# Conditioning products moved from VectorE to GpSimd, their row sums to ScalarE

## The chip, the cores and the metric

The kernel runs on one core of a Trainium2 chip. A core has five engines with instruction queues of their own: TensorE (PE in the profile, with its weight loads as PEld), VectorE (DVE), ScalarE (ACT), GpSimd (POOL) and SyncE (SP), which here only issues DMAs. Each queue runs in order; engines wait for one another by semaphores. The metric is the device time of one execution in microseconds, lower is better, as the median of several runs.

## The reference

A two-layer backbone over 256 latent and 256 context tokens of width 1024. Layer 0 mixes tokens with a bidirectional mLSTM, layer 1 with latent attention; a gated convolutional FFN follows each. What this change touches is the modulation: six vectors of width 1024 per layer and condition, from a matrix-vector product with the SiLU of a condition row. There are two conditions, `c` for the latents and `c_ctx` for the context.

```python
def _modulation(cond, w, b):
    m = jax.nn.silu(cond) @ w + b
    return jnp.split(m[:, None, :], 6, axis=-1)
...
        ml = _modulation(c, ada_w[i], ada_b[i])
        mc = _modulation(c_ctx[None, :], ada_w[i], ada_b[i])
        hl = _modulate(x, ml[0], ml[1])
...
        x = _layer_norm(ALPHA * x + ml[2] * yl, ln_g[i, 0], ln_b[i, 0])
```

## The kernel before

**Matrix products.** All weights are float32 and stream from memory in tiles of 128 x 1024. SyncE loads a tile (`raw`), ScalarE casts it to a high part (L345), VectorE subtracts that from the tile to get a low part (L368), and TensorE makes three products of high and low parts (L430, L433, L434). There are three buffers for the pair of parts (`NB = 3`, tile `w`); some tiles go to larger spare buffers instead (`wu`). A tile serves 24 matmuls of 512 columns in most stages and 12 in `mout`. The stages in order: start-up, `up`, `og`, the value products, `qk` (with the mLSTM heads' softmax-like work beside it), `mout`, the first FFN's `fin0` and its second product, layer 1's attention, `fin1`, `fout1`.

**The modulations.** Shift and scale of layer 0's mixer (chunks 0 and 1) are made in the start-up by TensorE. The rest are made later, in the background, without TensorE: the transposed matrix comes in tiles of 128 outputs x 1024 inputs (`ar`, L567), and for each condition VectorE multiplies a tile with the condition's SiLU row, broadcast to all partitions (`bc`), and accumulates along the row in the same instruction (`scalar_tensor_tensor` with `accum_out`, L544). The product itself goes to `junk` and is not read. One such instruction is a step. There are 128 steps on 80 tiles: chunks 2 and 3 (half) of layer 0 in `up` and `og`, 24 steps; the rest from `qk` to `fin0`, 104 steps. Layer 1's chunks 2 to 5 need only the latents' condition, so there a tile has one step, else two. After each chunk an addition of the bias follows (L549), and for the gates (chunks 2 and 5) a transposition and a store, since they are read back as rows.

**What sets the order.** The program is written as one sequence; a planner orders each engine's queue by that sequence and its own estimate of durations. Background work is kept in generators that are advanced at fixed places: `tick(n, n2)` advances the modulations by `n2` steps, kept as a running sum, after each weight tile. `ADA_U`, `ADA_T`, `ADA_Q`, `ADA_M` and `ADA_F` are these rates in `up`, `og`, `qk`, the first 22 tiles of `mout` and `fin0`. So that the planner does not run a step ahead of its place, `gate` (L559) lets ScalarE copy one element of the weight tile used last into the place that the step will write. `ar` tiles use three buffers (two of tag `ar`, one `ar1`), two loaded ahead at first. GpSimd otherwise issues DMAs (stores of `up`'s results, loads for heads and residuals) and makes two products at the very end (L1252, L1253).

Of the kernel before, what the change touches and what calls it, by code (L numbers as in the profile page):

```python
# [7 lines left out]
F32 = mybir.dt.float32  # L8
F32R = mybir.dt.float32r
I32 = mybir.dt.int32  # L10
AF = mybir.ActivationFunctionType
ALU = mybir.AluOpType
# [33 lines left out]

VE = {1: (3, 0), 2: (3, 0), 3: (3, 0)}

ADA_U, ADA_T, ADA_Q, ADA_M, ADA_F = 1.4, 1.3, 1.6, 0.6, 1.25

NUP = 5
# [345 lines left out]
class K:  # L401
# [127 lines left out]
    def ada_bg(self, l, c, k0, k1, nconds):  # L529


        nc = self.nc
        if c in (2, 5):
            v = self.adav
            col = v[:, 0:8 * nconds].rearrange("p (j k) -> p k j", k=8)
        else:
            col = self.modc[l, c][:, :, 0:nconds]
        for k in range(k0, k1):
            w = self.art.pop(0)
            self.ar_load()  # L540
            for j in range(nconds):
                o = self.pool.tile([128, 1024], F32, tag="junk", name="junk", bufs=1)
                self.gate(col[0:1, k, j:j + 1])
                nc.vector.scalar_tensor_tensor(o, w, 1.0, self.bc[j], op0=ALU.mult, op1=ALU.mult,  # L544
                                               accum_out=col[:, k, j:j + 1])
                yield
        b = self.smc("ada_c")[:, 48 * l + 8 * c + k0:48 * l + 8 * c + k1].unsqueeze(2).to_broadcast([128, k1 - k0, nconds])
        col = col[:, k0:k1]
        nc.vector.scalar_tensor_tensor(col, col, 1.0 if c in (1, 4) else 0.0, b, op0=ALU.add, op1=ALU.add)  # L549
        if c in (2, 5):  # L550
            t = self.pool.tile([128, 32], F32, tag="adat", name="adat", bufs=1)
            nc.vector.transpose(t, v)
            for q in range(4):
                nc.sync.dma_start(self.gd[l, c].rearrange("j (k q i) -> q (j k) i", q=4, i=32)[q, 0:8 * nconds],
                                  t[32 * q:32 * q + 8 * nconds])

    def gate(self, ap):

        self.nc.scalar.copy(ap, self.st.last[0:1, 0:1].bitcast(F32))  # L559
# [10 lines left out]
    def ada_all(self, items):  # L570

        nc = self.nc
        self.bc = []
        for j in range(2):
            r = self.pool.tile([128, 1024], F32, tag="acc", name="bc", bufs=2)
            self.gate(r[0:1, 0:1])
            nc.sync.dma_start(r, self.a["crow"][j:j + 1, :].to_broadcast([128, 1024]))
            self.bc.append(r)
        self.arq = [(l, c, k) for l, c, k0, k1 in items for k in range(k0, k1)]
        self.art, self.nar = [], 0  # L580
        for _ in range(2):
            self.ar_load()
        for _ in range(2):
            yield
        for r in self.bc:
            nc.scalar.activation(r, r, AF.Silu)  # L586
        yield
        for l, c, k0, k1 in items:
            yield from self.ada_bg(l, c, k0, k1, 2 if l == 0 or c < 2 else 1)
        self.bc = None  # L590


# [1770 lines left out]
```

## Time and profile before

| what | value |
|---|---|
| median of 3 runs | 1346.83 us (1346.54 to 1347.15) |
| span of the profiled execution, first to last instruction | 1345.3 us |
| TensorE, VectorE, ScalarE, GpSimd busy | 99%, 79%, 53%, 11% of the span |
| mean granted clock of TensorE | 0.998 |
| steps of the modulations (L544) | 128, the first at 63.0 us, the last at 866.2 us |

The profiled execution's own time is not listed apart from its span; the median of the runs lies 1.5 us above the span. Busy times of two engines overlap, so shares do not add up. Matmuls are pipelined, so a busy TensorE is judged by the distance between the starts of two matmuls. In a group's row stand the line, engine, operation, tiles and shapes, count, busy us, mean ns of one, and behind the second bar the engine's idle time before it with what ended it.

### The profile page before, as it was taken

What the parts mean: (1) busy time and instruction counts of PE and PEld (TensorE: products, weight loads), DVE (VectorE), ACT (ScalarE), POOL (GpSimd) and SP (SyncE); (2) the same over time, 40 slices, a digit from 0 to 9 for tenths busy, and PEclk for the clock granted to TensorE, in tenths of its full rate; (3) what the DMA queues carried; (4) which work ended last, traced back from release to release, by engine and by line L of the source; (5) the groups of instructions that cost most, each with busy time, mean ns of one, the idle gap of its engine ahead of it and who ended that gap; (6) DMA issues with size and microseconds to landing.
All of it is one profiled execution on the core that took longest, in us unless ns stands there. A gap on an engine that the chain in (4) does not pass through costs nothing.

```text
span 1345.3 us, 18750 instructions
## 1 busy us (share of the span) xinstructions
PE 1334.9 (99%) x6659; PEld 1120.2 (83%) x6659; DVE 1059.0 (79%) x1745; ACT 711.7 (53%) x1252; POOL 141.5 (11%) x236
## 2 busy tenths in 40 slices
PE   9999999999999999999999999999999999999997
PEld 5777888888888888888898888888888998988886
DVE  4798656678688696897979977758899889898874
ACT  4765444445744546474644334333566767676660
POOL 0222000011101011020002011111000002000100
PEclk9999999999999999999999999999999999999999
DMA  9988848889686384776628989967866437376750
GB/s 364 330 277 279 281 163 248 233 272 307 235 281 230 102 255 149 228 292 222 215 86 261 328 260 286 282 181 184 300 223 194 157 104 219 127 212 189 263 189 32
DMA packets 99885, 304.02 MB, mean 226 GB/s; under 512 B 12312, under 2 KB 25112, under 8 KB 99712
## 3 DMA queue, kind: packets, MB, share of 16 engines
q1 hardware_dynamic: 62992, 218.65, 48.6%
q0 software_dynamic: 26000, 66.75, 17.9%
q10 hardware_dynamic: 10800, 17.44, 3.6%
q8 instruction: 52, 0.85, 0.3%
q14 instruction: 41, 0.34, 0.1%
HBM read 272.21 MB, written 42.12 MB: 234 GB/s over the span
## 4 chain that ended last, share of the span: by engine, by line
PE 97%; DMA 1%; DVE 1%; ACT 0%; issue 0%; SPq 0%; DVEq 0%; ACTq 0%
PE fin L1503 8%; PE tok L430 6%; PE tok L434 6%; PE tok L433 6%; PE fin L433 6%; PE fin L434 6%; PE y L433 6%; PE fin L430 6%; PE y L434 6%; PE y L430 6%; PE qk L430 4%; PE qk L433 4%; PE qk L434 4%; PE up L718 2%; PE up L430 2%; PE up L434 1%
## 5 line engine op out<-in xcount | busy, mean ns | idle before, releaser
L368 DVE TENSOR_TENSOR w<-raw,w 128x1024 fp32r<-128x1024 f32 (+2 forms) x286 | 343.2, 1203 | 131.9 <-ACT w L345 129.7
L345 ACT CAST w<-raw 128x1024 fp32r<-128x1024 f32 (+2 forms) x286 | 296.2, 1037 | 282.4 <-PE tok L434 77.8
L544 DVE SCALAR_TENSOR_TENSOR junk<-ar,bc 128x1024 f32<-128x1024 f32 x128 | 156.1, 1219 | 5.2 <-ACT bc L586 2.3
L433 PE MATMUL fin<-h,w 128*128 128x512 f32 (+1 forms) x370 | 139.6, 377 | 0.0
L430 PE MATMUL fin<-h,w 128*128 128x512 f32 (+1 forms) x370 | 139.5, 377 | 0.0
L434 PE MATMUL fin<-h,w 128*128 128x512 f32 (+1 forms) x370 | 139.3, 377 | 0.0
L1503 PE MATMUL fin<-h,w 128*128 128x512 f32 (+1 forms) x636 | 111.1, 337 | 0.0
L1503 PEld LDWEIGHTS fin<-h,w 128*128 128x128 f32 x636 | 97.6, 190 | 13.2
L430 PE MATMUL qk<-xc,w 128*128 128x512 f32 x256 | 100.2, 391 | 0.0
L434 PE MATMUL qk<-xc,w 128*128 128x512 f32 x256 | 99.8, 390 | 0.0
L433 PE MATMUL qk<-xc,w 128*128 128x512 f32 x256 | 99.6, 389 | 0.0
L433 PEld LDWEIGHTS fin<-h,w 128*128 128x128 f32 x370 | 69.6, 188 | 13.0
L430 PEld LDWEIGHTS fin<-h,w 128*128 128x128 f32 x370 | 69.6, 188 | 12.9
L434 PEld LDWEIGHTS fin<-h,w 128*128 128x128 f32 x370 | 69.6, 188 | 12.6
L434 PEld LDWEIGHTS qk<-xc,w 128*128 128x128 f32 x256 | 48.0, 188 | 10.1
L430 PEld LDWEIGHTS qk<-xc,w 128*128 128x128 f32 x256 | 48.1, 188 | 9.8
L433 PEld LDWEIGHTS qk<-xc,w 128*128 128x128 f32 x256 | 48.1, 188 | 9.8
L430 PE MATMUL tok<-w,hT 128*128 128x512 f32 x128 | 49.9, 390 | 0.0
L433 PE MATMUL tok<-w,hT 128*128 128x512 f32 x128 | 49.8, 389 | 0.0
L434 PE MATMUL tok<-w,hT 128*128 128x512 f32 x128 | 49.8, 389 | 0.0
L735 ACT ACTIVATE fg<-fg 128x512 f32<-128x512 f32 (+1 forms) x44 | 23.1, 525 | 50.0 <-DVE fg L733 43.9
L368 DVE TENSOR_TENSOR wu<-raw,wu 128x1024 fp32r<-128x1024 f32 (+1 forms) x37 | 43.8, 1203 | 3.5 <-ACT wu L345 3.2
(486 smaller groups left out, 3125.7 us busy)
## 6 DMA issues: line engine op xcount, KB each, us to landing
raw<-in_ws SPq DMA_DIRECT2D x282, 512.0 KB, 4.5
ar<-in_adaT SPq DMA_DIRECT2D x80, 512.0 KB, 6.0
t4d<-in_ws POOLq DMA_DIRECT2D x20, 512.0 KB, 9.1
adaw<-in_ada SPq DMA_DIRECT2D x16, 512.0 KB, 8.0
zr<-fd ACTq DMA_DIRECT2D x33, 128.0 KB, 4.6
xmd<-xr POOLq DMA_DIRECT2D x16, 256.0 KB, 4.4
xcd<-cv POOLq DMA_DIRECT2D x16, 256.0 KB, 4.9
xs<-xmd POOLq DMA_DIRECT2D x16, 256.0 KB, 6.0
```

Of the source, the lines that this page charges most:

```text
L345: self.cast = k.nc.scalar.copy(h[:, :cols], src)
L368: i = self.k.nc.vector.tensor_sub(l[:, :n], src, h[:, :n])
L430: q = mm(out, w[0], x[0], start=start, stop=False, skip_group_check=on)
L433: mm(out, w[0], x[1], start=False, stop=False, skip_group_check=on)
L434: mm(out, w[1], x[0], start=False, stop=stop, skip_group_check=on)
L544: nc.vector.scalar_tensor_tensor(o, w, 1.0, self.bc[j], op0=ALU.mult, op1=ALU.mult, accum_out=col[:, k, j:j + 1])
L718: nc.tensor.matmul(ps[m], wk[i][:, c], hT[k][:, j], start=made[m] == 0, stop=made[m] == 23)
L735: nc.scalar.activation(tmp[:, :n], tmp[:, :n], AF.Silu)
L1503: self.nc.tensor.matmul(ps[:, 0:256] if x else ps, w[x][:, k * 128:(k + 1) * 128], h[:, 0:256] if x else h, start=i == 0 and not k0, stop= ...
```

## The change

Each step's product is made by GpSimd (`tensor_tensor` multiply), and its row sum by ScalarE (`activation` with Identity and `accum_out`, in place on the product). The sum of a step is written into the program two steps later: `pend` holds products not yet summed, and `ada_flush(1)` sums all but the last of them before the next product. Even steps write their product to `junk`, behind a gate; odd steps write it in place over the `ar` tile, without a gate. A tile whose last step wrote to `junk` is free after the product, at the next flush; one written in place is free after its sum; only then is the next `ar` load issued. Three tiles instead of two are loaded ahead. `ada_end` holds the part of `ada_bg` that follows a chunk's last step and is called when that step's sum has been issued. Two rates change: `ADA_Q` from 1.6 to 1.5, `ADA_M` from 0.6 to 1.0.

```diff
-ADA_U, ADA_T, ADA_Q, ADA_M, ADA_F = 1.4, 1.3, 1.6, 0.6, 1.25
+ADA_U, ADA_T, ADA_Q, ADA_M, ADA_F = 1.4, 1.3, 1.5, 1.0, 1.25
...
-        for k in range(k0, k1):
-            w = self.art.pop(0)
-            self.ar_load()
-            for j in range(nconds):
-                o = self.pool.tile([128, 1024], F32, tag="junk", name="junk", bufs=1)
-                self.gate(col[0:1, k, j:j + 1])
-                nc.vector.scalar_tensor_tensor(o, w, 1.0, self.bc[j], op0=ALU.mult, op1=ALU.mult,
-                                               accum_out=col[:, k, j:j + 1])
-                yield
...
+        for k in range(k0, k1):
+            for j in range(nconds):
+                self.ada_flush(1)
+                if j == 0:
+                    w = self.art.pop(0)
+                if self.nst % 2:
+                    o = w
+                else:
+                    o = self.pool.tile([128, 1024], F32, tag="junk", name="junk", bufs=1)
+                    self.gate(o[0:1, 0:1])
+                nc.gpsimd.tensor_tensor(o, w, self.bc[j], op=ALU.mult)
+                free = j == nconds - 1
+                if free and self.nst % 2 == 0:
+                    self.nfree += 1
+                    free = False
+                self.nst += 1
+                self.pend.append((o, col[:, k, j:j + 1], free, (l, c, k0, k1, nconds) if (k, j) == (k1 - 1, nconds - 1) else None))
+                o = None
+                yield
...
+    def ada_flush(self, keep):
+
+        while len(self.pend) > keep:
+            o, col, free, end = self.pend.pop(0)
+            self.nc.scalar.activation(o, o, AF.Identity, accum_out=col)
+            self.nfree += free
+            if end is not None:
+                self.ada_end(*end)
+        o = None
+        while self.nfree:
+            self.nfree -= 1
+            self.ar_load()
...
-        for _ in range(2):
+        self.pend, self.nst, self.nfree = [], 0, 0
+        for _ in range(3):
             self.ar_load()
...
+        yield
+        self.ada_flush(0)
```

More of the change, by code (lines that the diff above doesn't have):

```diff
@@ L533, in ada_bg, with ada_end @@
         if c in (2, 5):
-            v = self.adav
+            col = self.adav[:, 0:8 * nconds].rearrange("p (j k) -> p k j", k=8)
+        else:
+            col = self.modc[l, c][:, :, 0:nconds]
+        for k in range(k0, k1):
[5 more added lines that the diff above has]
+                    o = w
+                else:
+                    o = self.pool.tile([128, 1024], F32, tag="junk", name="junk", bufs=1)
[9 more added lines that the diff above has]
+                yield
+    def ada_end(self, l, c, k0, k1, nconds):
+        nc, v = self.nc, self.adav
+        if c in (2, 5):
             col = v[:, 0:8 * nconds].rearrange("p (j k) -> p k j", k=8)
```

## The prediction

> **What bounds the kernel now.** I read the page first, then what TensorE waited for, then its pace.
>
> ```profile
> span 1345.3 us, 18750 instructions
> PE 1334.9 (99%) x6659; PEld 1120.2 (83%) x6659; DVE 1059.0 (79%) x1745; ACT 711.7 (53%) x1252; POOL 141.5 (11%) x236
> PE 97%; DMA 1%; DVE 1%; ACT 0%; issue 0%; SPq 0%; DVEq 0%; ACTq 0%
> ```
> ```profile
> PE idle L655 <- DVE adav L497: 1.5, 1, 1.5
> PE adar L509 <- DMA adaw<-in_ada: 0.5, 1, 0.5
> PE up L718 <- DVE hT L693: 0.3, 1, 0.3
> PE y L433 <- DVE w L368: 0.2, 1, 0.2
> ```
> ```profile
> 739.82 0.39 PE L433 MATMUL fin<-h,w 128*128 128x512 f32 x1
> ...
> 751.84 0.39 PE L430 MATMUL fin<-h,w 128*128 128x512 f32 x1
> ```
>
> The second fence is the whole list of TensorE's waits: 2.5 us, of which only the last, 0.2 us, could concern a weight made late. The third is the first and last of 54 matmuls: 12.02 us over 53 steps, one matmul per 0.227 us while each lasts 0.39, so they overlap and the stream has no holes. TensorE sets the end; whatever the other engines are spared is worth 0.2 us at most, whatever they are charged is free until a weight comes late.
>
> How full the other engines are, in the stages in which the modulations run (matmul by up; by og; by qk; first and second part of mout; first product of the ffn). Columns: stretch, length, then busy us (count) of PE, PEld, DVE, ACT, POOL, clock, DMA share, GB/s:
>
> ```profile
> 63.00:110.00 47.00, 47.00 (x216) 37.51 (x215) 42.45 (x64) 30.60 (x59) 10.25 (x19) 1.00 0.85 273
> 110.00:151.00 41.00, 41.00 (x189) 32.55 (x188) 34.74 (x70) 21.12 (x42) 9.10 (x17) 1.00 0.89 306
> 352.00:577.00 225.00, 225.00 (x1052) 187.14 (x1052) 180.84 (x340) 112.34 (x225) 23.99 (x45) 1.00 0.65 213
> 577.00:615.00 38.00, 38.00 (x183) 31.55 (x182) 31.87 (x74) 24.30 (x54) 9.69 (x18) 1.00 0.65 239
> 615.00:649.00 34.00, 34.00 (x162) 28.21 (x161) 29.73 (x47) 17.55 (x26) 0.54 (x1) 1.00 0.58 206
> 689.00:867.00 178.00, 178.00 (x823) 148.84 (x822) 155.10 (x252) 75.20 (x137) 28.82 (x40) 1.00 0.88 267
> ```
>
> TensorE is busy in all of every stretch at full clock; VectorE is the fullest helper, GpSimd nearly idle.
>
> **The change part by part.** The rows that price it, from the groups by shape:
>
> ```profile
> L544 DVE SCALAR_TENSOR_TENSOR junk<-ar,bc 128x1024 f32<-128x1024 f32 x128 | 156.1, 1219 | 5.2 <-ACT bc L586 2.3 <-DMA ar<-in_adaT 1.5
> L544 DVE DVE_READ_ACCUMULATOR junk<-ar,bc 128x1 f32 x128 | 10.7, 83 | 0.0
> L559 ACT COPY mod<-w 1x1 f32<-1x1 f32 x78 | 12.3, 185 | 0.9
> L586 ACT ACTIVATE bc<-bc 128x1024 f32<-128x1024 f32 x4 | 4.2, 1062 | 2.8 <-DMA bc<-in_crow 2.8
> L1188 ACT ACTIVATION_READ_ACCUMULATOR jk<-oh 128x1 f32 x16 | 3.0, 187 | 0.0
> L345 ACT CAST w<-raw 128x1024 fp32r<-128x1024 f32 x272 | 285.8, 1053 | 271.6 <-PE tok L434 77.8 <-PE fin L434 72.2 <-PE y L434 46.1
> L368 DVE TENSOR_TENSOR w<-raw,w 128x1024 fp32r<-128x1024 f32 x272 | 331.5, 1222 | 128.0 <-ACT w L345 125.8 <-DMA raw<-in_ws 1.5
> ```
>
> *Removed from VectorE:* 128 products with their accumulator reads, 156.1 + 10.7 = 166.8 us. On TensorE's path: nothing, or the 0.2 us above.
>
> *Added to ScalarE:* 128 sums, 1.062 + 0.187 = 1.25 us each, 160 us in all; half of the 128 one-element gates go (64 x 0.185 = 11.8 us). A table load beside the Identity has no row of its own; L728 runs Identity 22 times between as many Silus of L735:
>
> ```profile
> L728 ACT ACTIVATE fg<-fin,sm 128x512 f32<-128x512 f32 x22 | 17.0, 773 | 1.1 <-PE fin L434 1.1
> L735 ACT ACT_TABLE_LOAD x2 | 2.6, 1283 | 0.2 <-DVE fg L733 0.2
> ```
>
> Two loads for 44 changes of function: I take none. If each sum brought one, 1.28 us more, mout's casts would be overrun at once.
>
> *Added to GpSimd:* 128 products. The trace has two products of half the size, shown with what VectorE did around them:
>
> ```profile
> 1334.56 0.68 DVE L1230 SCALAR_TENSOR_TENSOR z<-xres,z 128x512 f32<-128x512 f32 x1
> 1336.33 0.43 DVE L1230 SCALAR_TENSOR_TENSOR z<-xres,z 128x256 f32<-128x256 f32 x1
> ```
> ```profile
> 1334.98 1.43 POOL L1252 TENSOR_TENSOR z<-z,gr 128x512 f32<-128x512 f32 x1 [61.09 <-ACT z L1251]
> 1336.48 1.42 POOL L1253 TENSOR_TENSOR z<-z,br 128x512 f32<-128x512 f32 x1
> ```
>
> Upper size: 2 x 1.42 = 2.84 us. Both products began while VectorE was inside an op with two SBUF inputs, 0.26 us before its end (1335.24 - 1334.98) and 0.28 (1336.76 - 1336.48). If that overlap was waiting, a free product takes 1.15, and a whole one 2.30. I take 2.30 plus waiting, since the overlaps agree to 0.02 us; no row shows a product beside an idle VectorE, so 2.84 stays the other end. On the page GPSIMD Engine Reference, 3.1, the Trainium skill gives 4497 ns for 2048 elements; half, 2.25 us, is my estimate by that page, and the sum below would be 0.6 us smaller by it.
>
> *Steps by stage.* The pacing constants give 24 steps in up and og as before; some 45 in qk (32 ticks x 1.5, less three opening ones); 22 in mout (one per weight: 10 to 615, 12 after; now 4 and 5, two records each in the rows below); 37 in the ffn. VectorE's time in L544 in the two parts of mout:
>
> ```profile
> 577.00:615.00 38.00, 4.39 (x8) 1.00 0.65 239
> 615.00:649.00 34.00, 6.14 (x10) 1.00 0.58 206
> ```
>
> GpSimd's busy time by stage, 2.30 to 2.84 each on top of its row: up (14) 42 to 50 of 47 us; og (10) 32 to 38 of 41; qk 128 to 152 of 225; mout 33 to 38 of 38 and 28 to 35 of 34; ffn 114 to 134 of 178. ScalarE: up 30.6 + 14 x 1.25 - 0.9 = 47.2 of 47, og 33 of 41, qk 163 of 225, mout 24.3 + 12.5 + 0.4 = 37.2 of 38 and 17.6 + 15 = 32.6 of 34, ffn 117 of 178. So up and mout become brim-full, the rest has room.
>
> *The waits added.* A sum waits on ScalarE for its product two steps back; behind it in that queue stand the casts of the weights (L345), for these VectorE's subtraction, for that TensorE. How early a weight is there now in mout, where TensorE takes 12 x 0.227 = 2.72 us for one:
>
> ```profile
> 625.35 1.05 ACT L345 CAST w<-raw 128x1024 fp32r<-128x1024 f32 x1 [1.44 <-PE y L434]
> ```
> ```profile
> 626.44 1.23 DVE L368 TENSOR_TENSOR w<-raw,w 128x1024 fp32r<-128x1024 f32 x1 [0.35 <-ACT w L345]
> ```
>
> With three buffers the cast starts when TensorE leaves a weight and the result is wanted two weights later: 625.35 + 5.44 - 627.67 = 3.1 us early. In up, og, qk and the ffn a weight lasts 24 matmuls, 5.44 us, and the same sum gives 10.88 - 2.32 = 8.6 us. In up this covers the overflow (0.2 us on ScalarE, up to 3 on GpSimd): nothing on the path there.
>
> The ar loads stay 80; a buffer comes back some two steps later, behind the sum, and SP's queue holds the raw loads behind it.
>
> ```profile
> ar<-in_adaT SPq DMA_DIRECT2D x80, 512.0 KB, 6.0
> ```
>
> Three buffers of two steps are six steps; four are held, two are left for 6.0 us: 7.3 us in qk, 5.4 in mout. There a product is up to 0.6 us late, inside the two-step allowance. With one condition, in the ffn, a tile written in place is held three steps and its successor has one, 5.44 / 1.25 = 4.35 us: 1.7 us late, for which GpSimd's idle third has room; raw loads run three buffers ahead. POOL's own DMAs (xmd, vr, aB) are issued up to one product, 2.8 us, later; TensorE's list of waits names none of their tiles, so I take nothing, and 2.8 us a time where one is just in time.
>
> *The sum.* Left is the second part of mout, with its own groups of VectorE:
>
> ```profile
> L368 DVE TENSOR_TENSOR w<-raw,w 128x1024 fp32r<-128x1024 f32 x12 | 14.6, 1218 | 3.2 <-ACT w L345 3.2
> L1230 DVE SCALAR_TENSOR_TENSOR z<-xres,z 128x512 f32<-128x512 f32 x4 | 2.7, 676 | 0.0
> ```
>
> So 12 weights at 2.72 us, each with one product and one subtraction of 1.22. If they overlap freely: 2.84 a weight against 2.72, 1.4 us behind after 12, inside 3.1: nothing. If a product and an op with two SBUF inputs exclude each other: 2.30 + 1.22 = 3.52, so 12 x 0.80 = 9.6 us behind, plus the layer norm's ops there (the four of L1230 with two SBUF inputs, 2.7). Against it stand 3.1 us of weight lead and 2 x 2.72 - 2.30 = 3.1 that a product may be late before its sum is: 9.6 + 2.7 - 6.2 = 6.1 at full exclusion; with the lead used up before by a full first part, 12. Elsewhere even full exclusion fits: in qk 45 x 2.30 + at most 41 x 1.22 (225 / 5.44 weights) are 154 of 225 us, in the ffn 37 x 2.30 + 33 x 1.22 are 125 of 178. I take exclusion because of the two overlaps, and a little under its 6.1, since the sums' waits and the casts' own waits for TensorE fall partly together: 5 us. 1345.3 + 5 - 0.2 = 1350; the runs lie 1.5 us above the span (1346.83), so 1352.
>
> The Trainium skill says this outright: SBUF — State Buffer, "Who interferes with whom": a VectorE instruction with two SBUF inputs contends with a GpSimd instruction that reads SBUF, and the later one blocks for the whole instruction. The two overlaps agree; where they are chance, the page alone would stand for the 5 us.
>
> **The rivals.**
> (1) *The cover holds, no change:* VectorE's work and the products overlap, or the planner spreads the steps. For it: VectorE gives up 166.8 us, in mout 12 x 1.3 = 15.6 us of what the constants would now ask of it; 3.1 us of lead everywhere. Against it: brim-full rows. It decides if subtraction and product run at once in mout: then 1.4 us meet 3.1 of lead. Time 1346.8 + 0 to 1.5: 1347.5.
> (2) *Faster:* weights come earlier and TensorE's last holes close. Against it: holes of 0.2 us. Time 1346.6; more than 0.2% would need another order of TensorE's own work.
> (3) *A DMA at the head of GpSimd's queue.* It starts when a buffer comes free, and may sit there long:
>
> ```profile
> POOL vr L1133 <- PE hnT L1198: 79.0, 2, 43.4
> ```
> A product behind it holds its sum, that one the casts: 43.4 - 8.6 = 35 us, once 1382. It decides if the order puts products behind that DMA; while GpSimd had nothing else, waiting there cost nothing, so the row doesn't say.
>
> **How the numbers follow.** Forecast 0.50, rival 1 0.41, rival 2 0.05, rival 3 0.04. The forecast's own range is 1349.6 (the bound of what can be told from no change, 0.2% or 2.7 us) to 1360 (12 us, and one over). The whole range starts at 1346.3 to hold nearly all of rival 1, and ends at 1360; it leaves out rivals 2 and 3 and a tenth of the others. Slower 0.50 + 0.04 = 0.54, same 0.41, faster 0.05.
>
> **What would show it.** Products near 2.3 us alone and 3 and more beside subtractions, and L368 longer or later beside them, show the exclusion. TensorE's new waits should be "y" on "DVE w L368" between 577 and 670, about 5 us. If that stretch keeps its 0.227 us pace, the forecast is wrong and rival 1 holds; if the holes lie in up, the 8.6 us of lead was not there; if they lie in qk behind one long wait of a sum, it is rival 3.

## The result and the profile after

The changed kernel takes 1522.53 us (median of 4 runs, 1517.96 to 1524.65) against 1346.95 beside it: 1.130 times as long, with an interval of 1.128 to 1.132. The prediction, 1352 us, had the sign and 5 of the 176 us.

The page after: span, busy times, shares of the chain that ended last.

```profile
span 1522.9 us, 18764 instructions
PE 1391.1 (91%) x6659; PEld 1144.8 (75%) x6659; DVE 1028.4 (68%) x1489; ACT 839.8 (55%) x1444; POOL 489.4 (32%) x364
PE 34%; POOL 10%; issue 7%; DVE 4%; ACT 3%; DMA 3%; DVEq 0%; POOLq 0%; ACTq 0%
```

Three things are to be seen. TensorE has holes (91% busy instead of 99%), and yet no helper is near full. TensorE's own busy time rose by 56.2 us (1334.9 before) for the same 6659 matmuls, so the holes are only 121.4 of the 177.6 us. And VectorE, which gave up 166.8 us, lost only 30.6: 1059.0 - 166.8 = 892.2 was due, 1028.4 is there, 136 us too many.

What TensorE waits for now (us in total, times, longest):

```profile
PE PT L1147 <- DVE W L1134: 32.2, 5, 14.9
PE fin L427 <- ACT w L342: 17.5, 12, 2.9
PE sc L427 <- ACT qk L441: 16.7, 4, 13.1
PE fin L431 <- DVE w L365: 12.4, 18, 3.3
...
PE y L430 <- DVE w L365: 6.3, 4, 2.7
```

The wait that the prediction named, `y` on VectorE's `w`, is the last of these, 6.3 us. The first was not on its list: `PT`, the transposes of the heads' weights `W`.

The same six stretches as before the change, by their matmuls (length, then busy us of PE, PEld, DVE, ACT, POOL, clock, DMA share, GB/s):

```profile
63.70:118.00 54.30, 49.74 (x216) 38.37 (x214) 22.90 (x29) 39.46 (x72) 39.48 (x29) 0.97 0.60 207
118.00:177.50 59.50, 46.66 (x187) 33.81 (x188) 39.54 (x53) 32.59 (x61) 36.43 (x25) 0.94 0.61 203
384.80:661.90 277.10, 237.92 (x1052) 195.69 (x1051) 153.53 (x232) 157.71 (x289) 154.79 (x91) 0.93 0.51 164
661.90:725.00 63.10, 42.23 (x182) 34.75 (x181) 44.43 (x73) 37.11 (x76) 33.95 (x30) 0.81 0.54 194
725.00:776.20 51.20, 40.46 (x162) 31.11 (x161) 35.05 (x36) 29.85 (x49) 35.44 (x13) 0.90 0.51 170
816.30:1045.00 228.70, 198.61 (x823) 154.01 (x822) 145.47 (x171) 109.44 (x185) 122.23 (x76) 0.95 0.70 205
```

Every stage with steps is longer, also qk and the ffn, for which the prediction had room; after the last step (1020 us) nothing more is lost.

**The size of the pieces was right.** Products and sums by groups, and the products' least, median and longest duration:

```profile
L544 POOL TENSOR_TENSOR junk<-ar,bc 128x1024 f32<-128x1024 f32 x64 | 182.2, 2848 | 202.8 <-ACT junk L585 196.3 <-ACT bc L613 6.4
L544 POOL TENSOR_TENSOR ar<-ar,bc 128x1024 f32<-128x1024 f32 x64 | 169.2, 2643 | 29.1 <-DMA ar<-in_adaT 25.2 <-issue 0.4
L574 ACT ACTIVATE junk<-junk 128x1024 f32<-128x1024 f32 x64 | 67.9, 1061 | 164.5 <-POOL junk L544 164.5
L574 ACT ACTIVATE ar<-ar 128x1024 f32<-128x1024 f32 x64 | 67.8, 1059 | 95.6 <-POOL ar L544 95.6
```
```profile
L544 POOL TENSOR_TENSOR junk<-ar,bc x64: 2359/2732/3752, 65.1 to 1017.1; 128x1024 f32<-128x1024 f32 x64
L544 POOL TENSOR_TENSOR ar<-ar,bc x64: 2342/2410/4677, 69.5 to 1019.9; 128x1024 f32<-128x1024 f32 x64
```

A free product takes 2.35 us, a sum 1.06 plus its read. But the third and fourth rows show 260 us in which ScalarE stood still before a sum, waiting for its product.

**Exclusion, seen directly.** VectorE and GpSimd around three products (start, duration):

```profile
843.75 2.63 DVE L1705 TENSOR_TENSOR fs<-fg 128x256 f32<-128x256 f32 x1
...
856.07 3.42 DVE L365 TENSOR_TENSOR w<-raw,w 128x1024 fp32r<-128x1024 f32 x1
...
753.79 0.68 DVE L1258 TENSOR_TENSOR z<-y,gate 128x512 f32<-128x512 f32 x1
```
```profile
843.68 2.42 POOL L544 TENSOR_TENSOR ar<-ar,bc 128x1024 f32<-128x1024 f32 x1
...
855.47 2.93 POOL L544 TENSOR_TENSOR ar<-ar,bc 128x1024 f32<-128x1024 f32 x1
...
753.39 2.70 POOL L544 TENSOR_TENSOR ar<-ar,bc 128x1024 f32<-128x1024 f32 x1
```

The first operation, 0.43 us elsewhere, began 0.07 us after a product and ended 0.28 after it (846.38 against 846.10). The subtraction began 0.60 us after its product and ended 1.09 after it: it was held to the product's end and then took nearly its usual 1.22. The third ran inside a product and took its usual 0.68: its `y` is in PSUM.

**The sums' place in the queue.** ScalarE and GpSimd in the ffn:

```profile
861.10 0.17 ACT L585 COPY junk<-w 1x1 f32<-1x1 f32 x1
867.42 1.06 ACT L574 ACTIVATE junk<-junk 128x1024 f32<-128x1024 f32 x1 [6.15 <-POOL junk L544]
...
870.85 1.03 ACT L342 CAST w<-raw 128x1024 fp32r<-128x1024 f32 x1
```
```profile
861.76 1.75 POOL L1550 DMA_DIRECT2D x1d<-z  x3 [3.36 <-DVE z L1549]
864.29 0.54 POOL L1550 DMA_DIRECT2D x1d<-z  x1 [0.79 <-DVE z L1549]
864.85 2.54 POOL L544 TENSOR_TENSOR junk<-ar,bc 128x1024 f32<-128x1024 f32 x1
```

The next thing in ScalarE's queue after a product's gate is that same product's sum; so it is for 42 of the 64 gates, and 115 of the 128 sums began before the next product did. The program writes a sum two steps later. The planner put it earlier in the queue, presumably where its own estimate had the product ready; that estimate stands in no trace. ScalarE stands still for 6.15 us, the cast of a weight in the queue behind starts 9.6 us after the gate's end, and TensorE waits 1.46 us for that cast. This wait is one of the longest, and only 2.54 us of it are the product: before it GpSimd issued four stores of `x1d`, which waited for VectorE. Of all 260 us, 231 passed while the awaited product itself was running.

### The profile page after: what moved, and what is told of

It is laid out like the page before. It is cut to its first block, busy times and chain, and to the rows that moved or that the text cites. A ratio compares the mean times of both kernels' runs of the same rounds, so it can differ in the third digit from the quotient of the medians.

```text
span 1522.9 us, 18764 instructions
## 1 busy us (share of the span) xinstructions
PE 1391.1 (91%) x6659; PEld 1144.8 (75%) x6659; DVE 1028.4 (68%) x1489; ACT 839.8 (55%) x1444; POOL 489.4 (32%) x364
## 4 chain that ended last, share of the span: by engine, by line
PE 34%; POOL 10%; issue 7%; DVE 4%; ACT 3%; DMA 3%; DVEq 0%; POOLq 0%; ACTq 0%
PE fin L1532 7%; POOL junk L544 5%; POOL ar L544 4%; PE y L430 4%; PE y L431 4%; PE y L427 4%; DMA ar<-in_adaT 2%; PE fin L431 2%; PE fin L427 2%; PE fin L430 2%; PE y L1375 1%; ACT w L342 1%; DVE w L365 1%; DMA aB<-ad 1%; PE fin L1468 1%
## 5 line engine op out<-in xcount | busy, mean ns | idle before, releaser
L365 DVE TENSOR_TENSOR w<-raw,w 128x1024 fp32r<-128x1024 f32 (+2 forms) x286 | 365.2, 1281 | 189.5 <-ACT w L342 188.8
L544 POOL TENSOR_TENSOR junk<-ar,bc 128x1024 f32<-128x1024 f32 x64 | 182.2, 2848 | 202.8 <-ACT junk L585 196.3
L544 POOL TENSOR_TENSOR ar<-ar,bc 128x1024 f32<-128x1024 f32 x64 | 169.2, 2643 | 29.1 <-DMA ar<-in_adaT 25.2
L427 PE MATMUL fin<-h,w 128*128 128x512 f32 (+1 forms) x370 | 145.7, 394 | 17.7 <-ACT w L342 17.5
L574 ACT ACTIVATE junk<-junk 128x1024 f32<-128x1024 f32 x64 | 67.9, 1061 | 164.5 <-POOL junk L544 164.5
L431 PE MATMUL fin<-h,w 128*128 128x512 f32 (+1 forms) x370 | 146.4, 396 | 12.4 <-DVE w L365 12.4
L430 PE MATMUL fin<-h,w 128*128 128x512 f32 (+1 forms) x370 | 144.1, 390 | 0.0
L574 ACT ACTIVATE ar<-ar 128x1024 f32<-128x1024 f32 x64 | 67.8, 1059 | 95.6 <-POOL ar L544 95.6
L1532 PE MATMUL fin<-h,w 128*128 128x512 f32 (+1 forms) x636 | 111.1, 337 | 0.0
L1532 PEld LDWEIGHTS fin<-h,w 128*128 128x128 f32 x636 | 97.6, 190 | 13.1
L427 PE MATMUL qk<-xc,w 128*128 128x512 f32 x256 | 101.6, 397 | 2.0 <-ACT w L342 2.0
L431 PE MATMUL qk<-xc,w 128*128 128x512 f32 x256 | 100.7, 393 | 1.1 <-DVE w L365 1.1
L430 PE MATMUL qk<-xc,w 128*128 128x512 f32 x256 | 100.7, 393 | 0.0
L427 PEld LDWEIGHTS fin<-h,w 128*128 128x128 f32 x370 | 72.2, 195 | 36.0 <-ACT w L342 23.5
L431 PEld LDWEIGHTS fin<-h,w 128*128 128x128 f32 x370 | 72.4, 196 | 34.3 <-DVE w L365 21.2
L430 PEld LDWEIGHTS fin<-h,w 128*128 128x128 f32 x370 | 72.3, 195 | 13.6
L427 PE MATMUL tok<-w,hT 128*128 128x512 f32 x128 | 52.9, 413 | 11.9 <-ACT w L342 7.0
L430 PE MATMUL tok<-w,hT 128*128 128x512 f32 x128 | 52.5, 411 | 4.9 <-DVE w L365 4.9
```

Source lines behind the costliest of these rows:

```text
L365: i = self.k.nc.vector.tensor_sub(l[:, :n], src, h[:, :n])
L427: q = mm(out, w[0], x[0], start=start, stop=False, skip_group_check=on)
L430: mm(out, w[0], x[1], start=False, stop=False, skip_group_check=on)
L431: mm(out, w[1], x[0], start=False, stop=stop, skip_group_check=on)
L544: nc.gpsimd.tensor_tensor(o, w, self.bc[j], op=ALU.mult)
L574: self.nc.scalar.activation(o, o, AF.Identity, accum_out=col)
```

## The experiments

Where the time went, by stage: each matmul's start against the same matmul's in the kernel before, summed over the stages (us). The value products count with `og`. "Time" is the median of the runs; the kernel before ran beside each group and stood at 1346.95 to 1347.32.

| kernel | time | up, og | qk | mout | ffn |
|---|---|---|---|---|---|
| changed | 1522.5 | 32.8 | 52.1 | 42.4 | 50.7 |
| products by VectorE | 1350.0 | 0.1 | 0.3 | 0.7 | 2.0 |
| no sums | 1475.8 | 8.3 (and 29.5 at the start) | 35.5 | 32.0 | 22.7 |
| fills for products | 1389.6 | 0.5 | 10.2 | 17.2 | 16.8 |
| late sums | 1443.2 | 11.3 | 37.5 | 30.4 | 18.0 |
| late sums, fills | 1355.4 | 0.1 | 2.7 | 5.7 | 0.0 |
| late sums, half products | 1383.5 | 0.9 | 13.3 | 21.1 | 0.6 |

### Who makes the product

```diff
-                nc.gpsimd.tensor_tensor(o, w, self.bc[j], op=ALU.mult)
+                nc.vector.tensor_tensor(o, w, self.bc[j], op=ALU.mult)
```

> The changed kernel with one edit: the 128 products are made by VectorE again (a plain product of 1024 columns, no sum), the sums stay on ScalarE two steps later, with the same buffers, gates and rates. Before 1347, after 1522. Theories: (T1) exclusion: a GpSimd product and a VectorE subtraction shut each other out, which lengthens VectorE's work by some 136 us and makes the weights late; (T2) the sums stand in ScalarE's queue right behind their product's gate, wait there 2 to 7 us for a 2.4 to 2.9 us product, and the casts stand behind them; (T4) it is the plain load of 128 sums, 160 us, on ScalarE, whoever makes the product. T4 expects 1480 to 1522 here, with TensorE waiting for casts as after. T1 expects 1347 to 1360: VectorE is back near 892 + 128 x 1.2 = 1046 us. T2 expects an intermediate time, 1350 to 1400: the product takes 1.2 us instead of 2.4 to 2.9 and stands in the same queue as the subtractions, so ScalarE's waits for products fall from 260 us to under 130.

Measured: 1349.97 us, ratio 1.002 (1.0008 to 1.0031).

```profile
PE 1336.7 (99%) x6659; PEld 1119.8 (83%) x6659; DVE 1057.9 (78%) x1617; ACT 836.7 (62%) x1444; POOL 141.6 (11%) x236
```

ScalarE carries the same 837 us as in the changed kernel, and VectorE is as full as before, at a cost of 3 us. The plain load of 128 sums is not the cause. The loss needs the product on GpSimd. ScalarE still waited 84 us before sums here, and that alone cost next to nothing.

### No sums

```diff
+        nc.vector.memset(col[:, k0:k1], 0.0)
...
-            self.nc.scalar.activation(o, o, AF.Identity, accum_out=col)
```

> The changed kernel without the 128 sums on ScalarE (left out: the modulations then are their bias alone; a memset of the columns takes their place). Products, gates, loads and rates stay. T1 (exclusion of products and VectorE's operations) expects most of the loss to stay, 1450 or more, since all products still run beside the subtractions: mean product 2.6 to 2.9 us, VectorE near 1000 us. T2 (sums waiting at the head of ScalarE's queue) and T4 (ScalarE's plain load) expect 1347 to 1365. If the gate of the junk buffer (ScalarE writes into it ahead of the product, GpSimd waits 196 us for it) carries the coupling by itself, 1400 to 1500.

Measured: 1475.76 us (ratio 1.0957, 1.0925 to 1.0989). Of its loss, 29.5 us arose before the first step, from the edit itself: with no sum to wait for, the first bias addition moved to the front of VectorE's queue and waited there 27 us for its operand. The second row is that delay on TensorE:

```profile
PE PT L1147 <- DVE W L1134: 36.2, 5, 11.7
PE up L747 <- DVE hT L722: 27.5, 1, 27.5
```

The stages with steps lose 98 us, with no sum in any queue. So more than half of the 176 us arises without the sums. The time lies in the range of the theory of the gate, too; the section "Both" decides on it.

### Fills in place of products

```diff
-                nc.gpsimd.tensor_tensor(o, w, self.bc[j], op=ALU.mult)
+                nc.gpsimd.memset(o, 0.0)
+                nc.gpsimd.memset(o, 0.0)
+                nc.gpsimd.tensor_tensor(o[:, 0:8], w[:, 0:8], self.bc[j][:, 0:8], op=ALU.mult)
```

> The changed kernel with each product on GpSimd replaced by two fills of the same output tile and a product of its first 8 columns (left out: the products, so the sums are of 8 columns only). GpSimd is kept busy but reads next to nothing of SBUF; sums, gates, loads and rates stay. T1 (exclusion) expects 1347 to 1370 and VectorE back near 890 to 900 us, if a fill does not shut VectorE out. T2 and T4 expect 1450 or more if the pair of fills lasts about as long as a product (2.4 us); if it lasts less than 1.5 us the run tells T1 from T4 alone, and T2 expects 1350 to 1400.

Measured: 1389.59 us (1.0317, 1.0281 to 1.0354). The two fills and the short product take 0.97 + 0.96 + 0.35 = 2.28 us, close to a free product's 2.35, and GpSimd is as busy (31%).

```profile
PE 1350.2 (97%) x6659; PEld 1126.1 (81%) x6659; DVE 925.1 (67%) x1489; ACT 838.3 (60%) x1444; POOL 426.4 (31%) x620
```

VectorE is back at 925, and its subtraction at 1222 ns. A GpSimd instruction of the same length that reads next to nothing of SBUF holds nothing up. Neither theory alone gave the time: 42 us stay, and ScalarE still waits 129 us for the product.

### Sums behind the newest cast

```diff
-            self.nc.scalar.activation(o, o, AF.Identity, accum_out=col)
+            i = self.nc.scalar.activation(o, o, AF.Identity, accum_out=col)
+            self.behind(i, [self.st.cast])
```

> The changed kernel with one edit: each sum is put in ScalarE's queue behind the newest cast of a weight at the moment it is issued, that is, about two steps behind its product, as the change says; everything else stays. T2 (the sums stand right behind their products and hold the casts) expects 1347 to 1420. T1 (exclusion) and T4 (plain load) expect 1480 to 1522, with VectorE's busy time still near 1028 us.

Measured: 1443.19 us (1.0715, 1.0684 to 1.0746), between the two theories. The page and TensorE's waits:

```profile
PE 1361.8 (94%) x6659; PEld 1135.1 (79%) x6659; DVE 1074.5 (75%) x1489; ACT 838.5 (58%) x1444; POOL 479.3 (33%) x364
```
```profile
PE PT L1148 <- DVE W L1135: 37.7, 6, 12.4
PE fin L431 <- DVE w L365: 9.7, 7, 2.4
PE y L430 <- DVE w L365: 5.7, 3, 3.1
```

ScalarE's wait for products fell from 260 to 36 us, and the waits for casts are gone from TensorE's list. What is left ends on VectorE, which now carries 1074.5 - 892.2 = 182 us of holds. The stages lose 97 us, as without any sums: two ways of taking the sums out leave the same remainder.

### Both

> Both former edits at once: fills in place of the products (left out: the products, but for 8 columns), and each sum behind the newest cast. Fills alone left 42 us of the loss of 176, the later sums alone left 97. If the loss has just these two causes, exclusion of VectorE by products and casts queued behind waiting sums, nothing is left here: 1346 to 1352. If there is a third (the gate of the junk buffer, the ar loads that come later, GpSimd's own DMAs issued behind a product), more than 10 us stays: 1357 to 1390, with TensorE still waiting for it.

Measured: 1355.35 us (1.0064, 1.0041 to 1.0087). So 168 of the 176 us go with these two causes together. They aid each other: late sums save 34 us where GpSimd makes fills (1389.6 to 1355.4), but 79 where it makes products (1522.5 to 1443.2). Exclusion by itself is 1443.2 - 1355.4 = 88 us. The gates are still in this kernel, and GpSimd waits 124 us for them; so the gate of `junk` by itself costs no more than some of the 8 us that stay. Those 8 us lie in the first part of mout (5.4), where the prediction had ScalarE brim-full at 37.2 of 38 us, and in qk (2.7).

### How exclusion gets to 88 us

All runs of this part but two stand on the kernel with late sums (1443.2). First each product was cut into four instructions:

```diff
-                nc.gpsimd.tensor_tensor(o, w, self.bc[j], op=ALU.mult)
+                for q in range(4):
+                    s = slice(256 * q, 256 * q + 256)
+                    nc.gpsimd.tensor_tensor(o[:, s], w[:, s], self.bc[j][:, s], op=ALU.mult)
```

> Each sum behind the newest cast as before, and each product made in four instructions of 256 columns. From the 128x8 product (0.32 us) and the whole one (2.35 us) a quarter should take some 0.8 us, so a product 3.3 us, 40% more of GpSimd. The kernel with late sums and whole products took 1443. If the loss comes from the length of one hold (a VectorE operation that begins in a product is held to its end, up to 2.35 us, and everything behind it in VectorE's queue with it), a hold is at most 0.8 us now: 1350 to 1395, VectorE's held time under 90 us of the 180. If it is the sum of the occupied time (the port is taken 128 times a whole product, and VectorE's queue is too full to give it up), it gets worse: 1443 to 1480.

Measured: 1452.07 us (1.078, 1.0742 to 1.0818). A free quarter takes 0.71 us. VectorE's holds fell from 182 to 138 us, yet TensorE lost 10 us more, and ScalarE's wait for the longer products rose from 36 to 73. Shorter holds did not help, but the run changes two things at once, so it doesn't settle why.

Then half the dose:

```diff
-                nc.gpsimd.tensor_tensor(o, w, self.bc[j], op=ALU.mult)
+                nc.gpsimd.tensor_tensor(o[:, 0:512], w[:, 0:512], self.bc[j][:, 0:512], op=ALU.mult)
+                nc.gpsimd.memset(o[:, 512:1024], 0.0)
+                nc.gpsimd.memset(o[:, 512:1024], 0.0)
```

> Each sum behind the newest cast; the product is made of the first 512 columns only, and two fills of the other 512 keep GpSimd about as long as before (left out: half of each product). With whole products the time was 1443, with fills alone 1355, so products cost 88 us. If this goes with the time for which they shut VectorE out, half of it is left: 1355 + 44 = 1399, between 1388 and 1410. If it goes with the number of collisions, whatever their length, most of it stays: over 1420. If a lead covers short holds and only long ones come through, under 1380.

Measured: 1383.48 us (1.0266, 1.0236 to 1.0296). Half the products cost 28 us of the 88, between the first expectation (1388 to 1410) and the last (under 1380), but very unevenly: the ffn falls from 18.0 to 0.6 and up with og from 11.3 to 0.9, while qk and mout keep 34 of 68. In those last two, TensorE waits for one thing above all:

```profile
PE PT L1150 <- DVE W L1137: 17.8, 4, 8.6
```

The lead of that chain could have been read from the kernel before. The last operations on `W`, and the transposes that need them, in mout:

```profile
584.45 0.61 DVE L1105 SCALAR_TENSOR_TENSOR W<-W,R 128x128 f32<-128x128 f32 x2
...
593.91 0.74 DVE L1105 SCALAR_TENSOR_TENSOR W<-W,R 128x512 f32<-128x512 f32 x1
```
```profile
584.96 0.60 PE L1118 MATMUL PT<-ident,W 128*128 128x128 f32 x4
...
594.80 0.41 PE L1118 MATMUL PT<-ident,W 128*128 128x128 f32 x2
```

593.91 + 0.74 = 594.65, and the transposes start at 594.80: 0.15 us early, where the weights are 3.1 to 8.6 us early. In qk the last transposes of the three heads start 0.48, 1.85 and 1.82 us after the last operation on `W`. The four waits of the fence above follow these leads: 8.6 us in the first head and 7.3 in mout, 0.99 and 0.93 in the other two. Before that last operation stand, for each head, over 20 more operations of VectorE on `W` and its divisors, most of a kind that a product holds. Two runs on the kernel before the change tested this lead, with nothing of the change in them. One delays the chain:

```diff
             nc.vector.reciprocal(R[:, 0:2 * nd], R[:, 0:2 * nd])
+            for _ in range(12):
+                nc.vector.tensor_scalar(R[:, 0:2 * nd], R[:, 0:2 * nd], 1.0, None, op0=ALU.mult)
```

> The kernel before, with nothing of the change: VectorE multiplies the tiny tile R by one, 12 times over, in each of the 12 groups of the decay weights W (12 x 12 x 0.155 = 22 us more of VectorE in all, 1.9 us in a group). In the trace of before the transposes of W start only 0.15 to 1.85 us after the last operation of its chain, in all five places. If this short lead is what the held operations of the changed kernel break, TensorE waits for W here too: each of the four heads is late by up to 3 x 1.9 less the lead, and the time is 1355 to 1375, the wait named being that of the transposes for W. If VectorE has slack in these chains, or only the leads of the weights matter: 1346 to 1349.

The other delays weights:

```diff
         i = self.k.nc.vector.tensor_sub(l[:, :n], src, h[:, :n])
+        if self.order[j][0][0] in ("qk", "mout") and j % 4 == 0:
+            self.k.nc.vector.tensor_sub(l[:, :n], src, h[:, :n])
+            i = self.k.nc.vector.tensor_sub(l[:, :n], src, h[:, :n])
```

> The kernel before, with every fourth subtraction of a qk or mout weight made three times over (16 weights or so, 2 x 1.22 us each, 39 us more of VectorE in all): a longer delay than that put into the chain of W, in the same stages, but on the weights. If the lead of the weights (8.6 us in qk, 3.1 in mout) covers a delay, as the prediction had it, 1346 to 1350. If VectorE's queue there is so full that any delay goes through to TensorE, be it through W or the weights, 1360 to 1390.

Measured: 1353.32 us (1.0046, 1.0023 to 1.0069) and 1354.88 us (1.0057, 1.0034 to 1.008). TensorE's waits for `W` in the first, and for a weight in the second:

```profile
PE PT L1120 <- DVE W L1107: 3.9, 3, 3.1
```
```profile
PE y L436 <- DVE w L368: 2.0, 1, 2.0
```

In qk, three heads' share of the first delay (some 15 of 20 us) cost TensorE 6.3 us, while 10 of the second's 16 weights, 24 of 39 us, cost 0.5: the place decides, and the weights' long lead does cover. In mout the other 6 cost 7.3 us, though each delay, 2.44 us, is less than the 3.1 us of lead: what the prediction counted for one weight did not cover there. The first run came out below its range. The planner sees an edit and plans again: the first head's second group of transposes stands 24 matmuls behind its first group there, 14 in the kernel before, so a part of the delay could not reach TensorE. Last, products were kept out of that chain, with whole and with half products (`self.hot` is set where a head's groups begin and cleared behind the last):

```diff
-        while self.acc2 >= 1:
+        m = 0
+        while self.acc2 >= 1 and m < 2 and not self.hot:
             self.step(self.bg2)
             self.acc2 -= 1
+            m += 1
```

> The changed kernel with each sum behind the newest cast, as before (1443 then), and no step of the modulations issued while a head's chain of W is being made; they are made up for afterwards, at most two a tick. If the holds cost what they do because they fall into that chain, TensorE's wait of 38 us for W goes to under 10, and the time to 1385 to 1425: the weights' waits stay, or grow a little where the steps are made up for. If place doesn't matter, 1435 to 1460, the waits only having other names.

> Half products as before (left out: half of each product), sums behind the newest cast, and no step issued while a head's chain of W is being made. Half products alone took 1383, with nothing lost in up, og and the ffn, 13 us in qk and 21 in mout, and a wait of 18 us for W; fills alone 1355. If what is left is the short lead of the chain of W, 1357 to 1370, with the wait for W under 5 us and qk's loss under 5. If the steps that are made up for cost as much elsewhere, 1378 to 1390.

Measured: 1430.19 us (1.0619, 1.0575 to 1.0663) against 1443.2, and 1374.31 us (1.0203, 1.0173 to 1.0232) against 1383.5. The waits of `PT` for `W` fell from 37.7 to 16.6 us and from 17.8 to 6.0, and qk's loss from 37.5 to 27.3 and from 13.3 to 6.4; 13 and 9 us came back. With whole products the stages outside qk lost about what they had lost before (mout 28.6 against 30.4, ffn 18.7 against 18.0), so the steps made up for afterwards cost little there; with half products up and og lost 3.6 us more. Both landed between their expectations: the short lead is a part, not the whole.

### Three smaller questions

The rates of before in the changed kernel:

```diff
-ADA_U, ADA_T, ADA_Q, ADA_M, ADA_F = 1.4, 1.3, 1.5, 1.0, 1.25
+ADA_U, ADA_T, ADA_Q, ADA_M, ADA_F = 1.4, 1.3, 1.6, 0.6, 1.25
```

> The changed kernel with the pacing constants of before (1.6 and 0.6 steps for qk and mout instead of 1.5 and 1.0). The loss of the changed kernel went with the steps, some 1.4 us for each of 128, in every stage. By this 1515 to 1530, with less of the loss in mout and more in the ffn. If mout's rate of one step a weight were the cause, as the prediction had it, over 25 of mout's 42 us go and do not come back in the ffn: under 1500.

Measured: 1512.99 us (1.1232, 1.1187 to 1.1278), just under its range. mout's loss falls from 42.4 to 16.9, as the second reading asked, but it comes back in part: qk's rises from 52.1 to 59.6, and 5.5 us arise behind the ffn, whose own loss stays (51.1). The rates moved the loss, and 10 of 176 us went.

Products by VectorE and late sums together:

> The product by VectorE (a plain product, no sum), the sum by ScalarE behind the newest cast. With VectorE's product and the sums where the changed kernel has them, 1350.0 was measured, 3 us over before. If these 3 us are casts behind waiting sums, they go: 1346 to 1348. If they are VectorE's load or the loads of ar, 1349 to 1351 again.

Measured: 1360.65 us (1.0101, 1.0072 to 1.0131), outside both ranges: 11 us slower than with the sums where the change has them. A late sum gives its `ar` tile back later, and VectorE now waits 21 us for tiles that an in-place step needs (13 in the first experiment). It was not followed further; the 3 us of the first experiment stay unexplained.

The loads of `aB`, from which `W` is made, taken out of GpSimd's queue, in the changed kernel and in that with late sums:

```diff
-            nc.gpsimd.dma_start(aB[d], self.ad[d, h:h + 1, :].to_broadcast([128, 512]))
+            nc.sync.dma_start(aB[d], self.ad[d, h:h + 1, :].to_broadcast([128, 512]))
```

> The changed kernel (1522) with one edit: the eight loads of aB, from which each head's weights W are made, are issued from SP's queue instead of GpSimd's. In the trace of before they are issued about 30 us ahead of their use, in that of the changed kernel 4 us, behind products that wait for their gate; VectorE waits 33.6 us for them, and TensorE's longest wait (14.9 us, for W) ends on the chain that starts there. If this is a third cause, VectorE's wait for aB goes to near 0, the wait for W from 32 to under 18 us and the time to 1485 to 1512. If VectorE is late for other reasons at that place, 1515 to 1530.

> The same edit on top of each sum behind the newest cast (1443 without it; there VectorE waits 14.7 us for aB). If late loads hold part of the wait of 38 us for W, 1415 to 1435; if that wait is exclusion alone, 1438 to 1448.

Measured: 1512.27 us (1.1227, 1.1185 to 1.127) and 1459.87 us (1.0838, 1.0807 to 1.087). VectorE's wait for these loads, in the changed kernel and with the edit:

```profile
DVE Am L1079 <- DMA aB<-ad: 33.6, 8, 8.9
```
```profile
DVE Am L1079 <- DMA aB<-ad: 23.5, 7, 8.5
```

In the changed kernel 10 us of the 176 went, and TensorE's wait for `W` fell from 32.2 to 21.7, but the loads are late in SP's queue as well; with late sums the edit costs 17. Whether the late loads are a third cause stays open; if so, a small one.

## Why the prediction was wrong, point by point

**Right: what bounds the kernel, and that nothing is gained.** With products by VectorE, ScalarE's extra 128 sums, gates and later loads moved the time by 0.2%: VectorE's 166.8 us were hidden work, and so was the room on ScalarE.

**Right: the prices.** 2.30 us for a free product was 2.35; 1.25 for a sum was 1.25; no table loads; 166.8 us off VectorE.

**Right: the mechanism of the forecast.** Two overlaps of 0.26 and 0.28 us were taken for exclusion, and it is exclusion. In the changed kernel and the one with late sums, operations of two SBUF inputs that began inside a product were held to the product's end, down to a 128x2 one of 0.16 us that took 2.35; the exceptions ran while the product itself was still being held. So were multiplications by a column with one full SBUF input (`W<-W,R`, 128x512: 2.6 us instead of 0.48). Operations with a PSUM input, the layer norm's statistics, reciprocals and fills were not. This is what the Trainium skill says (SBUF — State Buffer, "Who interferes with whom"): the later one of a GpSimd instruction that reads SBUF and a VectorE one with two SBUF inputs, or in a two-port mode, blocks for the whole instruction; `tensor_scalar` is listed there among those that can enter such a mode.

**Wrong: "Elsewhere even full exclusion fits: in qk ... 154 of 225 us, in the ffn ... 125 of 178".** This is the step that failed most. It added the products to the subtractions only. VectorE's queue runs in order, and behind a held operation everything stands. What VectorE gives up in each stage is its time in L544 before; the prediction shows it for the two parts of mout (4.39 and 6.14 us), and these are up, og, qk and the ffn:

```profile
63.00:110.00 47.00, 17.12 (x28) 1.00 0.85 273
110.00:151.00 41.00, 12.28 (x20) 1.00 0.89 306
352.00:577.00 225.00, 63.16 (x103) 1.00 0.65 213
...
689.00:867.00 178.00, 51.06 (x83) 1.00 0.88 267
```

VectorE's busy time less this, with a free product added for each step that the prediction counted, gives: up 42.45 - 17.12 + 14 x 2.35 = 58 of 47 us, og 46 of 41, qk 223 of 225, mout 51 of 38 and 52 of 34, ffn 191 of 178. Five of the six are over, by 60 us in all, and qk has next to no room. With half products (1.27 us free) up, og, qk and the ffn fit (43, 35, 175 and 151), and the parts of mout stay over (40 and 39). The experiments follow that line: with half products up, og and the ffn lose next to nothing, and mout keeps 21 of its 30 us. In qk they don't: half products lose 13 us there with 50 to spare, which the short lead of `W` explains in part. It is a sum made afterwards, and it counts operations that can overlap, so it bounds rather than explains; but it says that these stages have no room, and the prediction's said the opposite.

**Wrong: the cover.** "3.1 us of lead everywhere" and 8.6 in up, og, qk and the ffn were the leads of the weights. TensorE also waits for other things of VectorE, and `W` was 0.15 to 1.85 us early. In the changed kernel that wait is the longest, 32.2 us. The list of TensorE's waits did not name it, and the prediction took what isn't waited for now as having room. A lead that is just kept leaves no row among the waits.

**Wrong: "a sum waits on ScalarE for its product two steps back".** Mostly a sum waits for the product begun last: 42 of 64 stand right behind their own product's gate. The prediction took the place in the program for the place in the queue; the allowance of 3.1 us that came from it ("that a product may be late before its sum is") was not there. Undoing it gives 79 us of the 176.

**Left out: what a hole costs beside itself.** TensorE after two holes:

```profile
1001.31 0.51 PE L427 MATMUL fin<-h,w 128*128 128x512 f32 x1 [1.15 <-ACT w L342]
...
1002.57 0.50 PE L431 MATMUL fin<-h,w 128*128 128x512 f32 x1 [0.53 <-DVE w L365]
...
1003.55 0.63 PE L431 MATMUL fin<-h,w 128*128 128x512 f32 x1
1003.98 0.63 PE L427 MATMUL fin<-h,w 128*128 128x512 f32 x1
```

Behind the holes one matmul comes every 0.43 us instead of 0.227, for 3.4 us. The clock records of the whole execution hold 20 stretches at half clock, 122 us in all (before: only one, at the very end, 7.5 us; here that is the last of the 20), and TensorE's busy time is 56 us longer: a third of the loss. So a wait of 1.7 us here cost about 1.7 us more.

**The rivals.** No change and faster are out. The third, one long wait of a sum for a product behind a DMA, did not occur as priced: the longest wait of a sum is 6.8 us, and of the 260 us in 112 waits some 12 passed behind GpSimd's DMAs. That the second part of mout would bear it all fell too: with late sums it loses 13.5 us (0.2 with fills) where 5 were due, and that is 13.5 of 97.

## What to carry to other kernels

A product that goes to GpSimd was not free for VectorE here, 136 to 182 us of holds for 128 products, while fills were: where VectorE's operations have two SBUF inputs, price a GpSimd instruction that reads SBUF as time taken from VectorE's whole queue in that stage, and ask then whether the stage still fits. Read the lead of everything the bounding engine takes from the engines that are touched, also of what it doesn't wait for today. And where an in-order queue is filled by a planner, read the distance between producer and consumer from the queue, not from the program.

## What the runs showed of the hardware that was not expected

A hole of far less than 3.4 us brought the half clock: 1.15 and 0.53 us with two matmuls between them were enough at 1001 us, and the clock stayed halved for one stretch of 3.4 us; of the 20 stretches, 16 are 3.4 or 6.8 us long. All of them begin on one grid of 3.41 us. In the 3.41 us just before each of the 19 inside the run TensorE had stood idle for 1.66 us or more, in one hole or several; with less the clock never fell, and six times it stayed full with 1.67 to 1.93. The Trainium skill (TensorE: Matmul & The Clock Gate, "Part 1: The HAM clock gate") has the two rates and the window of 3.4 us, and the trace agrees with both; its rule of no idle gaps over some 3.4 us ("HAM oscillation — how this bites in real kernels") is too lenient by this trace. That a multiplication by a column with a single full SBUF input is held like one with two was not expected either.
